# Three edits to a hybrid decoder trunk: the queue that begins a running sum, the order of the attention's output products, and the tick of two heads' transposes

## The chip, the cores and the metric

The kernel runs on one core of one Trainium2 chip. The metric is the device time of one execution in microseconds (us). The core's engines run side by side, each through its own instructions in order: TensorE (PE, matrix products; its weight loads are shown as PEld), VectorE (DVE), ScalarE (ACT), GpSimd (POOL) and SyncE (SP). SP and POOL here do little but begin DMA transfers, each on a queue of its own: SP's is "q1 hardware_dynamic" in the profile, POOL's "q0 software_dynamic".

## What is computed

Two layers, 512 tokens of width 1024, float32. Layer 0 mixes tokens with dilated attention (three groups of eight heads), layer 1 with a gated recurrence; each is followed by a feed-forward block (FFN) of width 3072. Cut to what matters:

```python
def reference(x, ...):
    for layer in range(2):
        h = rms_norm(x, norm_mix_pre[layer])
        h = dilated_attention_mixer(h, ...) if layer == 0 else rglru_mixer(h, ...)
        x = x + rms_norm(h, norm_mix_post[layer])
        h = conv_ffn(rms_norm(x, norm_ffn_pre[layer]), w_up, conv_w, conv_b, w_down)
        x = x + rms_norm(h, norm_ffn_post[layer])
    return x

def dilated_attention_mixer(x, w_qkv, w_o, rel_bias):   # the end of it
    alpha = softmax(lses, axis=0)                       # over the three head groups
    o = sum(alpha[..., None] * outs, axis=0)
    return o.reshape(B, S, 1024) @ w_o                  # output products

def conv_ffn(x, w_up, conv_w, conv_b, w_down):
    u = causal_dwconv(x @ w_up, conv_w, conv_b)
    g, v = u[..., :3072], u[..., 3072:]
    return (gelu(g) * v) @ w_down
```

## The kernel before

Every product is done in three passes of TensorE, because each operand is split in two parts: ACT makes the high part (`whi` for weights, L253; `ahi` for activations, L184) and DVE the low part (`wlo`, L265; `alo`, L185). A pass has 128 by 512 products, and one weight half of 1 MB gives two "units" (a unit is one `whi` and one `wlo` tile; eight are held, `W_UNITS`).

Some products are done by a scheme that needs seven products of blocks where plain code needs eight, and for it sums of blocks of the weights: a "first" block is copied from memory into a tile named `sum`, and then further blocks are added to it in place by DMA transfers that accumulate. `add_up` (L298) issues both: the copy at L309, the accumulating ones at L311, all from POOL. POOL waits for one to land before it issues the next, because the next reads the tile that the former wrote. Plain blocks of weights are loaded by `load` (L317) into tiles named `raw`, from SP (L340). `plan` lists all weights in the order of their use; `loads` (L280) is called whenever a tile was read, first issues the loads that have a free tile, then the next step of a sum. The entries of `plan` that belong to the attention have numbers below `state["lagging"]` (L1733), the FFN's and the recurrence's lie above.

In each FFN, 16 products (`step`, L971, products at L633, tile `vq`) of the down projection are woven between the blocks of the up projection (tile `ps`, L436); their weights come as `value` loads and as sums, in the order that `down_quarters` (L1696) gives: load; first and sum; load; sum; load; sum; first and sum; and the same again for a second unit. The sums of the up projection (`w_seven`, L414) have firsts of their own. There are 16 firsts above `lagging`: four of the up and four of the down projection in each layer.

Work that is not tied to one product runs as a "side": a generator that is resumed at `tick()`, which is called after each piece of products; `yield n` lets n ticks go by. The loads' splitting is pumped at ticks too.

At the end of the attention, `rows_run` (L694) does the output products in the order of `LAST_ORDER`: pairs of token tiles (four of 128 tokens) and chunks of `w_o` (four of 256 rows, two heads each). Each of its 16 pieces has 12 matmuls and ends in a tick. The tiles' products collect in `acc` tiles, two PSUM banks for each token tile; PSUM has eight banks (`pp`, L133), and all tiles named `ps`, `vq`, `acc`, `PT`, `O`, `tr` take theirs from these eight. The last four heads (numbers 4 to 7) are still being finished in the first ticks: `strided` (L1352) scales the weights `L` (L1429), and for the last two heads, with `ahead` set, writes the shares to memory (L1442), reads them spread (L1364), turns `L` on TensorE (L1449, tile `PT`, two banks for a head), copies the turned tiles out on ACT (L1451), and makes `oT` (L1465 to L1470). `prep` splits `oT` into `ahi` and `alo` up to two pieces ahead of their products.

Of the kernel before, what the change touches and what calls it, by code (L numbers as in the profile page):

```python
# [53 lines left out]


LAST_ORDER = [
    ([0, 1], [0, 1, 2]), ([2], [0]), ([0], [3]), ([1], [3]), ([3], [0]), ([2, 3], [1]), ([2], [2, 3]), ([3], [2, 3]),
]

LOCAL_STEPS = [("l", 0, 1), ("l", 1, 0), ("l", 1, 1), ("l", 2, 0), ("l", 2, 1)]  # L60
# [35 lines left out]
def kernel(  # L96
# [28 lines left out]
    nc = tc.nc  # L125
# [12 lines left out]
    def nm(s):  # L138
        uid[0] += 1
        return f"{s}{uid[0]}"  # L140

    def gen(dt=F32, s="g"):
        return gp.tile([P, 512], dt, tag="g", name=nm(s))

    def psum(s="ps"):
        return pp.tile([P, 512], F32, tag="ps", name=nm(s))
# [41 lines left out]
    state = {"raw": 0, "free": RAW_BUFS, "at": 0, "live": 0, "next": 0, "rows": False, "hold": False, "slots": 4, "tick": 0, "lagging": 0}  # L188
# [91 lines left out]
    def loads():  # L280
        moved = True
        while moved:
            moved = False
            while state["raw"] < len(plan) and plan[state["raw"]][0] in ADDED:
                state["raw"] += 1
            if state["raw"] < len(plan):
                kind = plan[state["raw"]][0]
                if state["slots"] >= SLOTS[kind] if kind in SLOTS else state["free"]:
                    load()
                    moved = True  # L290
            while total["next"] < len(plan) and plan[total["next"]][0] not in ADDED:
                total["next"] += 1
            i = total["next"]
            if i < state["raw"] and total["open"] and after[i] in finished:
                add_up(i)
                moved = True

    def add_up(i):  # L298

        kind, kd, cols, srcs = plan[i]  # L300
        if total["tile"] is None or total["cols"] != cols:
            total["cols"] = cols
            total["tile"] = cp.tile([P, 512 // cols, 4, cols], F32, tag="gain", name=nm("sum"))
        tile_, at = total["tile"], 0
        part = tile_[:, int(kind[-1] == "1")]
        for src, m in srcs:
            dst = part[:, :, at : at + m]
            if kind[:5] == "first":
                nc.gpsimd.dma_start(dst, src)  # L309
            else:  # L310
                nc.gpsimd.dma_start(dst, src, accum_op=ALU.add)  # L311
            at += m
        raws[i] = tile_ if kind == "mix" else part
        since[i] = state["tick"]
        total["next"] += 1
# [762 lines left out]
    def attention(hT, post, pre, spill):  # L1078
# [201 lines left out]
        def to_dram(t, ms, name):  # L1280
            d = dp.tile([P, 512], F32, name=name)
            nc.sync.dma_start(strips(d)[:, :, ms, :], strips(t)[:, :, ms, :])
            return d

        def from_dram(d, ms):

            t = gen(s="PT")
            w = 32 * (ms.stop - ms.start)
            src = bass.AP(tensor=d.tensor, offset=d.offset + 32 * ms.start, ap=[[P, P], [32 * 512, 4], [1, w]])
            dst = t.rearrange("p (i c) -> p i c", i=4)[:, :, 32 * ms.start : 32 * ms.stop]  # L1290
            nc.sync.dma_start(dst, src)
            return t.rearrange("p (i m q) -> p m i q", i=4, m=4)
# [59 lines left out]
        def strided(h, hh, qks, v, ahead=None):  # L1352
# [4 lines left out]
            def local_out():  # L1357
                t = gen(s="ow")
                nc.sync.dma_start(t, o0[h])
                return t  # L1360

            def spread(d):
                t = gen(s="share")
                nc.sync.dma_start(t, bass.AP(tensor=d.tensor, offset=d.offset, ap=[[0, P], [1, 512]]))  # L1364
                return t
# [74 lines left out]
            if ahead:  # L1440
                yield 1
                nc.sync.dma_start(cd, c0)  # L1442
                yield 1
                share = spread(cd)
                for L in Ls:
                    ps = psum("PT")
                    for r in range(4):
                        c = slice(r * P, (r + 1) * P)
                        nc.tensor.transpose(ps[:, c], L[:, c], ident)  # L1449
                    pt = gen(s="PT")  # L1450
                    nc.scalar.activation(pt, ps, AF.Copy)  # L1451
                    pts.append(pt.rearrange("p (r u) -> p r u", r=4))
            else:
                yield 1
                placed = [to_dram(t, all_, f"std{h}{gi}") for gi, t in enumerate(turned)]
                nc.sync.dma_start(cd, c0)
                yield 2
                pts = [from_dram(d, all_) for d in placed]
                share, ow = spread(cd), local_out()
# [69 lines left out]
        for hp in range(4):  # L1529
# [4 lines left out]
            for j in range(4):  # L1534
                if j == 3 and hp:
                    by_residue(vrows[hp], v)
                if j == 1 and last:
                    prep(2)
                if j == 2 and last:
                    both = [(qs[:2], ks[:2])]  # L1540
                    heads = [strided(6 + hh, hh, both, v, True) for hh in range(2)]
                    for hh, g in enumerate(heads):
                        side(one(g), 1 + hh)
                feat_tiles(1, hT, lambda m, ps: sink(2 * j + m, ps), paired=False)
                step("s", hp, j)
            if not hp:
                by_residue(vrows[hp], v)
            if last:
                both.append((qs[2:], ks[2:]))
                for hh, g in enumerate(heads):  # L1550
                    next(g)
                for hh in (1, 0):
                    side(heads[hh], 1 + hh, first=True)
                prep(4)
                for t in range(4):
                    xs_sb[t] = load_x(t)
            else:
                both = [(qs[2 * g : 2 * g + 2], ks[2 * g : 2 * g + 2]) for g in range(2)]
                for hh in range(2):
                    side(strided(2 * hp + hh, hh, both, v), 1 + hh)  # L1560
# [294 lines left out]
```

## Time and profile before

| | us |
|---|---|
| median of 3 runs | 1408.19 (1405.84 to 1410.74) |
| profiled execution, its own time | 1408.95 |
| its span, first to last instruction | 1407.2 |
| PE busy | 1364.2 |
| DVE busy | 1053.5 |
| ACT busy | 671.9 |
| POOL busy | 123.5 |

The profile is of one execution. The span is divided by engine into busy time and idle time; an idle time is put down to what ended it. The attention ends at about 492 us of the span, layer 0's FFN runs from there to about 870, the recurrence to about 1025, and layer 1's FFN to the end.

### The profile page before, as it was taken

What the parts mean: (1) busy time and instruction counts of PE and PEld (TensorE: products, weight loads), DVE (VectorE), ACT (ScalarE), POOL (GpSimd) and SP (SyncE); (2) the same over time, 40 slices, a digit from 0 to 9 for tenths busy, and PEclk for the clock granted to TensorE, in tenths of its full rate; (3) what the DMA queues carried; (4) which work ended last, traced back from release to release, by engine and by line L of the source; (5) the groups of instructions that cost most, each with busy time, mean ns of one, the idle gap of its engine ahead of it and who ended that gap; (6) DMA issues with size and microseconds to landing.
All of it is one profiled execution on the core that took longest, in us unless ns stands there. A gap on an engine that the chain in (4) does not pass through costs nothing.

```text
span 1407.2 us, 18680 instructions
## 1 busy us (share of the span) xinstructions
PE 1364.2 (97%) x7109; PEld 1201.2 (85%) x7109; DVE 1053.5 (75%) x1838; ACT 671.9 (48%) x1125; POOL 123.5 (9%) x141
## 2 busy tenths in 40 slices
PE   8999999999998999998999999999999999999997
PEld 5888888888887899997878879888899997888886
DVE  6886483737585788877949689878979877968785
ACT  6334342423444554445535354579563445535351
POOL 1211011011010001000000020000000010000020
PEclk9999999999999999999999999999999999999999
DMA  8979669686838244573658775233153672758771
GB/s 247 238 219 280 171 186 256 204 204 160 283 128 289 88 151 110 162 193 90 194 160 195 199 209 180 90 120 120 61 165 82 174 206 65 187 165 216 185 219 60
DMA packets 179116, 243.10 MB, mean 173 GB/s; under 512 B 16632, under 2 KB 131840, under 8 KB 179026
## 3 DMA queue, kind: packets, MB, share of 16 engines
q1 hardware_dynamic: 143008, 172.23, 37.5%
q0 software_dynamic: 36016, 69.67, 23.6%
q8 instruction: 56, 0.92, 0.3%
q14 instruction: 34, 0.28, 0.1%
q10 hardware_dynamic: 2, 0.00, 0.0%
HBM read 218.23 MB, written 28.36 MB: 175 GB/s over the span
## 4 chain that ended last, share of the span: by engine, by line
DVE 29%; DMA 11%; ACT 9%; PE 5%; issue 5%; DVEq 0%; SPq 0%; ACTq 0%; POOLq 0%
DVE wlo L265 9%; DVE u L821 7%; DMA sum<-in_ffn_w_down_dram 5%; PE acc L436 4%; ACT whi L253 3%; DMA raw<-in_ffn_w_down_dram 2%; DMA raw<-in_ffn_w_up_dram 2%; ACT u L817 2%; DVE xb L1574 1%; ACT u L831 1%; DVE A L915 1%; DVE y L647 1%; DVE u L833 1%; DVE c L647 1%; DVE run L608 1%
## 5 line engine op out<-in xcount | busy, mean ns | idle before, releaser
L436 PE MATMUL ps<-hT,whi 128*128 128x512 f32 (+1 forms) x2528 | 696.9, 362 | 0.8 <-DVE hT L499 0.6
L436 PEld LDWEIGHTS ps<-hT,whi 128*128 128x128 f32 x2528 | 458.9, 190 | 57.5 <-issue 1.3
L436 PE MATMUL ps<-hT,wlo 128*128 128x512 f32 (+1 forms) x1264 | 456.3, 361 | 3.0 <-DVE wlo L265 3.0
L253 ACT ACTIVATE whi<-raw 128x1024 fp32r<-128x1024 f32 x233 | 239.1, 1052 | 149.5 <-DMA raw<-in_attn_w_qkv_dram 73.5
L265 DVE TENSOR_TENSOR wlo<-raw,whi 128x1024 fp32r<-128x1024 f32 x233 | 280.3, 1218 | 30.6 <-ACT whi L253 30.4
L436 PEld LDWEIGHTS ps<-hT,wlo 128*128 128x128 f32 x1264 | 239.6, 190 | 32.7 <-DVE wlo L265 5.0
L821 DVE SCALAR_TENSOR_TENSOR u<-ps,cols,u 128x511 f32<-128x511 f32 (+1 forms) x160 | 119.6, 747 | 88.3 <-ACT u L817 85.4
L633 PE MATMUL vq<-whi,A 128*128 128x512 f32 x448 | 140.5, 385 | 2.6 <-ACT A L922 2.6
L253 ACT ACTIVATE whi<-sum 128x1024 fp32r<-128x1024 f32 x68 | 70.7, 1049 | 142.4 <-DMA sum<-in_attn_w_qkv_dram 74.2
L265 DVE TENSOR_TENSOR wlo<-sum,whi 128x1024 fp32r<-128x1024 f32 x68 | 82.0, 1218 | 49.1 <-ACT whi L253 49.1
L436 PE MATMUL acc<-whi,ahi 128*128 128x512 f32 x256 | 98.8, 386 | 2.7 <-ACT ahi L184 2.7
L436 PE MATMUL acc<-whi,alo 128*128 128x512 f32 x256 | 97.9, 382 | 3.4 <-DVE alo L185 3.3
L633 PEld LDWEIGHTS vq<-whi,A 128*128 128x128 f32 x448 | 86.0, 192 | 16.0 <-ACT A L922 3.4
L436 PE MATMUL acc<-wlo,ahi 128*128 128x512 f32 x256 | 97.9, 383 | 1.5 <-DVE wlo L265 1.5
L633 PE MATMUL vq<-wlo,A 128*128 128x512 f32 x224 | 87.1, 389 | 9.6 <-DVE wlo L265 9.6
L831 ACT ACTIVATE u<-u 128x512 f32<-128x512 f32 x48 | 30.3, 631 | 111.4 <-DVE u L821 111.4
L817 ACT ACTIVATE u<-ps,cols 128x512 f32<-128x512 f32 x80 | 61.1, 764 | 4.7 <-PE ps L436 4.7
L633 PE MATMUL vq<-whi,T 128*128 128x512 f32 x192 | 59.7, 382 | 0.0
L436 PEld LDWEIGHTS acc<-whi,alo 128*128 128x128 f32 x256 | 48.6, 190 | 12.5 <-DVE alo L185 5.8
L633 PEld LDWEIGHTS vq<-wlo,A 128*128 128x128 f32 x224 | 43.1, 192 | 18.5 <-DVE wlo L265 12.4
L436 PEld LDWEIGHTS acc<-whi,ahi 128*128 128x128 f32 x256 | 48.7, 190 | 9.8 <-ACT ahi L184 3.3
L436 PEld LDWEIGHTS acc<-wlo,ahi 128*128 128x128 f32 x256 | 48.7, 190 | 9.6 <-DVE wlo L265 3.1
(246 smaller groups left out, 1799.2 us busy)
## 6 DMA issues: line engine op xcount, KB each, us to landing
raw<-in_ffn_w_up_dram SPq DMA_DIRECT2D x44, 1024.0 KB
raw<-in_attn_w_qkv_dram SPq DMA_DIRECT2D x25, 1024.0 KB
sum<-in_ffn_w_down_dram POOLq DMA_DIRECT2D x24, 1024.0 KB, 8.6
raw<-in_ffn_w_down_dram SPq DMA_DIRECT2D x16, 1024.0 KB
sum<-in_attn_w_qkv_dram POOLq DMA_DIRECT2D x24, 512.0 KB, 8.1
raw<-in_attn_w_qkv_dram SPq DMA_DIRECT2D x16, 512.0 KB
sum<-in_ffn_w_up_dram POOLq DMA_DIRECT2D x16, 512.0 KB, 6.8
raw<-in_lru_w_in_dram SPq DMA_DIRECT2D x8, 1024.0 KB
```

What stands on the lines that cost most here:

```text
L253: nc.scalar.activation(hi, raw, AF.Copy)
L265: nc.vector.tensor_tensor(lo, raw, hi.bitcast(F32), op=ALU.subtract)
L436: mm(dst, l[a], r[b], start=start and n == 0, stop=stop and n == 2)
L608: nc.vector.tensor_tensor(r[h], a, b[:, k], op=ALU.add if sg > 0 else ALU.subtract)
L633: mm(banks[u], act(a)[:, 2 * j + k, u * P : (u + 1) * P], woven(W[b][:, k, :]), start=(j, k, n) == (0, 0, 0), stop=(j, k, n) == (1, 1, 2),)
L647: nc.vector.tensor_tensor(dst[u], a[u], b[u], op=op)
L817: nc.scalar.activation(u, ps, AF.Identity, scale=cc[:, j : j + 1], bias=cc[:, 48 + j : 49 + j])
L821: nc.vector.scalar_tensor_tensor(u[:, d:], ps[:, : S - d], wc, u[:, d:], op0=ALU.mult, op1=ALU.add)
L831: nc.scalar.activation(u, u, AF.Gelu_apprx_tanh)
L833: nc.vector.tensor_tensor(gv[k], gv[k], u, op=ALU.mult)
L915: nc.vector.tensor_tensor(run[:, k], run[:, k] if prior is None else prior[k], src[k], op=ALU.add if sign > 0 else ALU.subtract,)
L1574: nc.vector.scalar_tensor_tensor(u[:, d:], ps[:, : S - d], wc, u[:, d:], op0=ALU.mult, op1=ALU.add)
```

## The change

Three edits:

- `LAST_ORDER`: the pieces of token tiles 0 and 1 with chunk 2 (heads 4 and 5) move from the fifth and sixth place to the seventh and eighth. Token tile 2 takes chunks 0 and 1 (heads 0 to 3) in the fifth and sixth place, and tile 3 takes both at the eleventh and twelfth. There are 16 pieces as before. Chunk 3 comes to tiles 0 and 1 at the ninth and tenth place (eighth and ninth before).
- `add_up`: the "first" copies of entries above `lagging` are issued from SP, not from POOL. Those of the attention stay on POOL, as do all accumulating transfers.
- `strided` with `ahead`: two ticks instead of one go by between the writing of the shares and their reading with the transposes. So the transposes of heads 6 and 7 come after the fourth and fifth piece, not after the third and fourth, and their `oT` one tick later too.

```diff
 LAST_ORDER = [
-    ([0, 1], [0, 1, 2]), ([2], [0]), ([0], [3]), ([1], [3]), ([3], [0]), ([2, 3], [1]), ([2], [2, 3]), ([3], [2, 3]),
+    ([0, 1], [0, 1]), ([2], [0, 1]), ([0, 1], [2]), ([0], [3]), ([1], [3]), ([3], [0, 1]), ([2], [2, 3]), ([3], [2, 3]),
 ]
@@ add_up
             if kind[:5] == "first":
-                nc.gpsimd.dma_start(dst, src)
+                (nc.gpsimd if i < state["lagging"] else nc.sync).dma_start(dst, src)
             else:
                 nc.gpsimd.dma_start(dst, src, accum_op=ALU.add)
@@ strided
             if ahead:
                 yield 1
                 nc.sync.dma_start(cd, c0)
-                yield 1
+                yield 2
                 share = spread(cd)
```

## Rows read from the trace of the kernel before

**Rows 1.** The page: busy time by engine, and what the slices moved.
```profile
PE 1364.2 (97%) x7109; PEld 1201.2 (85%) x7109; DVE 1053.5 (75%) x1838; ACT 671.9 (48%) x1125; POOL 123.5 (9%) x141
GB/s 247 238 219 280 171 186 256 204 204 160 283 128 289 88 151 110 162 193 90 194 160 195 199 209 180 90 120 120 61 165 82 174 206 65 187 165 216 185 219 60
```
**Rows 2.** PE's waits, 430 to 600 us: total us, times, longest.
```profile
PE acc L436 <- ACT ahi L184: 2.7, 2, 2.3
PE PT L1449 <- DVE L L1429: 2.3, 1, 2.3
```
**Rows 3.** PE's waits, 600 to 830 us.
```profile
PE vq L633 <- DVE wlo L265: 5.8, 3, 3.3
PE ps L436 <- DVE wlo L265: 2.1, 2, 1.6
PE vq L633 <- ACT A L922: 0.7, 1, 0.7
```
**Rows 4.** PE's waits, 1130 to 1380 us.
```profile
PE vq L633 <- DVE wlo L265: 3.8, 4, 1.6
PE vq L633 <- ACT A L922: 1.8, 1, 1.8
...
PE ps L436 <- DVE wlo L265: 0.9, 2, 0.6
```
**Rows 5.** Stretches: length, busy us of each engine (instructions), granted PE clock, DMA.
```profile
660.30:663.70 3.40, 3.40 (x10) 2.68 (x9) 3.14 (x6) 3.22 (x5) 1.28 (x1) 0.50 0.32 46
664.00:704.00 40.00, 40.00 (x187) 35.04 (x186) 37.22 (x55) 22.01 (x28) 2.08 (x2) 1.00 0.72 192
```
**Rows 6.** The chain of waits: start us, us (DMA: issue to landing), what.
```profile
615.87 10.68 DMA raw<-in_ffn_w_down_dram
...
698.47 6.30 DMA sum<-in_ffn_w_down_dram
...
705.17 13.22 DMA sum<-in_ffn_w_down_dram
...
727.74 9.38 DMA raw<-in_ffn_w_up_dram
...
1148.92 11.36 DMA raw<-in_ffn_w_down_dram
```
**Rows 7.** SP in order of time: start us, us, line, what it issues.
```profile
620.31 0.37 SPq L340 DMA_DIRECT2D raw<-in_ffn_w_up_dram  x1
...
688.78 0.37 SPq L340 DMA_DIRECT2D raw<-in_ffn_w_up_dram  x1
```
**Rows 8.** ACT in order of time; in brackets the idle time before, and its end.
```profile
644.52 1.04 ACT L253 ACTIVATE whi<-sum 128x1024 fp32r<-128x1024 f32 x1
...
688.51 1.06 ACT L253 ACTIVATE whi<-sum 128x1024 fp32r<-128x1024 f32 x1 [0.73 <-DMA sum<-in_ffn_w_down_dram]
...
694.06 1.06 ACT L253 ACTIVATE whi<-raw 128x1024 fp32r<-128x1024 f32 x1 [2.31 <-DMA raw<-in_ffn_w_up_dram]
...
808.13 1.06 ACT L253 ACTIVATE whi<-sum 128x1024 fp32r<-128x1024 f32 x1 [15.04 <-DMA sum<-in_ffn_w_down_dram]
...
1178.25 1.04 ACT L253 ACTIVATE whi<-sum 128x1024 fp32r<-128x1024 f32 x1
```
**Rows 9.** POOL in order of time, around the FFN's sums of layer 0.
```profile
608.41 0.79 POOL L309 DMA_DIRECT2D sum<-in_ffn_w_down_dram  x1 [13.37 <-DVE wlo L265]
...
679.89 1.30 POOL L311 DMA_DIRECT2D sum<-in_ffn_w_down_dram  x1 [18.28 <-DVE wlo L265]
...
793.80 1.27 POOL L311 DMA_DIRECT2D sum<-in_ffn_w_down_dram  x1 [6.21 <-DMA sum<-in_ffn_w_down_dram]
```
**Rows 10.** PE and ACT in order of time, at the attention's end.
```profile
451.43 1.63 PE L1449 MATMUL PT<-ident,L 128*128 128x128 f32 x8 [2.26 <-DVE L L1429]
...
453.38 0.63 ACT L184 ACTIVATE ahi<-oT 128x512 fp32r<-128x512 f32 x1 [4.40 <-DVE oT L1469]
453.91 1.07 ACT L1451 ACTIVATE PT<-PT 128x512 f32<-128x512 f32 x2
```

## The prediction

> **What bounds the kernel now.** I read the page first: PE is busy for 97% of the span, DVE for 75% [rows 1]. So at most the idle 43 us of PE are to be had, and the question is which of its waits the change touches. The waits of PE by stretch tell that. At the attention's end there are 2.7 us for ACT's split of activations, two waits with 2.3 the longest, and 2.3 us for DVE's scaling of a head's weights [rows 2]. In layer 0's FFN there are 8.6 us: 5.8 and 2.1 for the low parts of weights, 0.7 for an operand [rows 3]. In layer 1's there are 6.5 us of the same kinds [rows 4]. A long wait costs more than itself: after the one of 3.3 us PE ran 3.4 us at the lower of its two clocks, granted 0.50, that is 1.2 GHz; ten matmuls took what 16 take at 2.4 GHz (187 in 40 us, 0.214 us each) [rows 5]. That is another 1.7 us. There are three such dips behind waits, at 452, 660 and 1172 us, of which one row stands.
>
> The chain of waits then tells why the weights are late. ACT works strictly in order, so one split that waits for a transfer holds the convolutions behind it, and DVE, which waits for those. A load begun at 615.87 takes 10.68 us to land, its twin in layer 1 takes 11.36, the sum begun at 705.17 takes 13.22, a load at 727.74 takes 9.38 [rows 6]. A load of the same size with no other transfer beside it, begun at 688.78 [rows 7], is read from 694.06 on, just when it lands: 5.28 us [rows 8]. A sum alone takes 8.6 us, from 679.89 [rows 9] to 688.51; the slowest here 14.3, from 793.80 [rows 9] to 808.13 [rows 8].
>
> **Edit 1: 16 firsts on SP.** Nothing is added or removed; each first leaves POOL's queue (0.79 us of POOL [rows 9]) and takes 0.37 us of SP's [rows 7]. What counts is where it stands. The eight of the up projections cost nothing: where their weights are used PE waits for none (in layer 0 from 492 to 600 us, where [rows 2] has no wait for weights). A sum that came later than its lead would cost PE the difference. The eight of the down projection come in four kinds, once in each layer. Loads are issued ahead of a step of a sum in the same call, and SP's instructions run in order, so a first stands behind all loads written before it.
>
> (a) The first at 608.41 [rows 9] was written after the loads of 615.87 [rows 6] and 620.31 [rows 7], which wait for their tiles. POOL ran ahead of them; SP can't. The first is issued at about 620.7, 12 us later, and neither it nor its sum runs beside the load of 615.87 any more. This load then lands in 5.28 us instead of 10.68: 5.4 us earlier, and ACT and DVE gain that lead. The price is the sum. The load of 620.31 lands at 625.6; the first, next in the same queue, moves its 1.05 MB at the 289 GB/s of the best slice [rows 1] in 3.6 us and lands at 629.2; the sum is issued at about 629.6 and takes 8.6 to 14.3 us, say 11: it lands at 640.6 (638.2 to 643.9). ACT now comes to it at 644.52 without waiting [rows 8], then at 639.1. So 3.9 us of lead are left (5.4 to 0.6). PE's waits here are 0.7 and, 20 us on, 3.3 with the dip of 1.7 [rows 3, 5]. The first goes; PE then needs 4.0 of lead to lose the other. Worth 5.7 in full, 0.6 with the least lead; I take 5.2. Layer 1: the load gains 11.36 − 5.28 = 6.1; its successor is issued 4.5 us behind it, as in layer 0, so the first lands at about 1162.3 and the sum at 1173.7 (1171.3 to 1177.0), where ACT comes at 1178.25 − 6.1 = 1172.2 [rows 6, 8]. The wait of 1.8 and its dip of 1.7 come before the sum and go; the wait of 1.6 [rows 4] then needs 5.1 of lead and finds 4.6 (6.1 to 1.3). I take 4.6; between 1.3 and 5.1.
>
> (b) The first at 698.47 took 6.30 us from POOL [rows 6]. SP's queue is empty then, so it starts at the same time and lands in 5.28: its sum begins 1.0 us earlier, and ahead of the load that now crowds it. Of 2.5 us of waits (5.8 less 3.3 [rows 3]) I take 2.0, between 1.0 and 2.5. In layer 1 POOL's first is quicker already, by 0.7 us; 0.8 of some 1.8, not under 0.4.
>
> (c) A first is written just after the load of 727.74, and POOL's copy runs beside that load. Behind it, the load lands in 5.28 instead of 9.38 [rows 6], and the 2.1 us of waits for its low part go [rows 3]; but the first lands 2.9 us later than now (727.74 + 5.28 + 3.6 against 727.25 + 6.3), and so its sum. PE takes that sum's product without a wait today, but no row shows by how much. I take 1.2, between −2.9 and 2.1; in layer 1 0.4 of 0.9 [rows 4], down to −2.9.
>
> (d) The last first, at 786 us, meets an empty SP queue again: its sum, for which ACT idles 15.04 us [rows 8], begins about a microsecond earlier. PE's waits behind it are split among many operands: 1.0 for both layers, between −1 and 2.
>
> The Trainium skill speaks against this edit, on the page "DMA: Bandwidth & Descriptors", section "Issuing engines are not separate DMA queues": transfers of all issuing engines interleave on the same 16 DMA engines, so that another issuer saves only the time to issue. The row agrees that they share (10.68 against 5.28 us); by that rule alone edit 1 would be worth nothing, and the rival "same" below is its case.
>
> **Edits 2 and 3: the attention's end.** Piece 3 waits 2.3 us for ACT [rows 2]; its operand and its place stay, so this wait stays. The wait of 2.3 us ahead of head 7's transposes [rows 10] is what the edits aim at: one more piece (12 × 0.214 = 2.6 us) comes ahead of them, on heads that are long ready. But the piece is tile 2's, and opens two more banks: six of eight are held by sums then, and the other two by head 6's turned weights. Head 7's transposes need these two back, and ACT frees them with the copies of 453.91. Those stand behind a split that waits for DVE until 453.38 [rows 10], and nothing moves that. So PE goes on at about 454.5 instead of 451.43; the second copy ends at 455.0, four more transposes take 0.8 us at most (half of 1.63), and PE is through at 455.7, one piece ahead. Now it has done the same work at 453.1 + 2.6 + 1.5 (most of the dip) = 457.2. That is 1.5 us gained; but the wait is then 2.5 us, and a dip behind it gives 1.7 back. The smaller wait for ACT (2.7 less 2.3 = 0.4 us [rows 2]) goes, since the table load no longer stands between head 7's output and its split. I take 1.0: 4.5 if no bank is waited for (2.3 + 1.7 + 0.4), −1.2 if the dip comes and the later ticks are late. Tile 0's and 1's norms start one piece later, and three pieces still cover their transposes; if that cover were gone, PE would wait for ACT as in [rows 2], 0.4 to 2.3 us. SP's instructions in `strided` are the same; the spread read, which waits for its write, no longer stands ahead of the other head's write.
>
> **Sum.** 5.2 + 4.6 + 2.0 + 0.8 + 1.2 + 0.4 + 1.0 + 1.0 = 16.2 us off the profiled execution's 1408.95: 1392.8. That execution is 0.8 us above the median of the three runs, so 1392 for a median. All best ends together give 24.6 us, 1384; all worst ends −4.7, 1413.
>
> **Rivals.** *Sums too late.* The lead of (a) is eaten by the later sum (14.3 us, as the slowest today), (b) to (d) give their low ends without a loss: 0.6 + 1.3 + 1.0 + 0.4 + 0.5 = some 4 to 6 us, 1403. For it: the sum comes 12 us later. Against: even then it lands before the time at which ACT comes today.
>
> *Same.* The transfers only share the engines, and whichever is begun first pays: the load still meets other traffic, DVE's own work (37.2 of 40 us busy behind the dip [rows 5]) refills every lead, and the attention's wait only moves. Then the time is 1407 to 1408. Against: the load of 615.87 has nothing left beside it until it lands. This is the case of the rule cited above.
>
> *Slower.* SP's queue hands out three transfers without overlap, 5.28 us each: in (a) the first lands 15.8 us behind the first load, at 631.7, and with a sum of 14.3 us at 646.4, later than ACT's 644.52 of today by 1.9; in layer 1 by about 1.1. In (c) the first lands at 738.3, 4.7 later than now; with a slack of 2 for PE there, each layer loses 2.7. Together 8.4 us, less the 1.4 of (b)'s low ends: 1415. It decides from the point at which the sum of (a) lands behind 644.5, 15 us after a first that lands at 629.2; no sum here took that long.
>
> **How the numbers follow.** The forecast (10 to 25 us off, 1384 to 1399): 0.62. Sums too late (1399 to 1404): 0.17. Same: 0.13. Slower: 0.08. A measurement of this kernel tells about 0.3%, 4.2 us, from no change: faster means below 1404, 0.79; same 0.14; slower 0.07. The range, 1384 to 1404, takes in the first two cases and so both ends of most unknown costs.
>
> **What would show it.** Right, if SP issues the first copies at about 620 and 1153 us; if the loads ahead of them land in 5 to 6 us instead of 10.68 and 11.36; if PE's waits of 0.7 and 3.3 us, 1.8 and 1.6 us, and both dips of the clock, are gone; if head 7's transposes wait for ACT's copies and not for DVE. Wrong, if ACT now waits for the sum that it reads at 644.52 for more than some 2 us, if the load's 10.68 us hardly shrink, or if SP's queue holds a first for long and the loads behind it come late.

## The result and the profile after

The changed kernel takes 1385.37 us in the median of three runs (1384.54 to 1386.12), where the kernel before took 1408.19 beside it. The ratio is 0.9837 with a 95% interval of 0.9808 to 0.9866: some 23 us less (18.9 to 27.0). The profiled execution took 1385.37 us, of which the span is 1383.6. In later runs the same two kernels gave 1383.87 and 1402.99, a ratio of 0.9864 (0.9831 to 0.9896), 19.1 us less (14.6 to 23.7). Both intervals hold 18.9 to 23.7 us.

The page: PE's busy time fell by 7.4 us against [rows 1] with the same 7109 instructions (two dips of its clock that went, below, are part of that), and POOL has 16 instructions fewer.

```profile
PE 1356.8 (98%) x7109; PEld 1200.9 (87%) x7109; DVE 1052.2 (76%) x1838; ACT 670.7 (48%) x1125; POOL 111.1 (8%) x125
```

PE's waits from 430 to 600 us, to be read against [rows 2] (total us, times, longest):

```profile
PE tr L489 <- DVE xs L481: 3.4, 2, 2.6
PE acc L436 <- ACT ahi L184: 2.4, 1, 2.4
PE PT L1449 <- ACT PT L1451: 1.5, 1, 1.5
```

The wait for DVE ahead of PT has gone, and one for ACT's copies stands there. But a line that [rows 2] does not have, 3.4 us for `xs`, is larger than what went. From 600 to 830 us, against the 8.6 us of [rows 3], this is the whole list:

```profile
PE vq L633 <- DVE wlo L265: 2.5, 2, 1.6
```

From 1130 to 1380 us no wait is listed any more, where [rows 4] had 6.5 us. So the feed-forward layers gave the time, and the attention did not.

Their transfers, in the chain of waits (start, us from issue to landing); against [rows 6] the load of 615.87 takes 5.64 us instead of 10.68, but the sum of 705.17 is as slow as it was:

```profile
616.16 5.64 DMA raw<-in_ffn_w_down_dram
...
693.06 6.40 DMA sum<-in_ffn_w_down_dram
700.11 13.08 DMA sum<-in_ffn_w_down_dram
```

SP, POOL and ACT in order of time at the first of these places, against [rows 7 to 9]: the first transfer stands behind both loads on SP, POOL issues the sum at 629.11, and ACT comes to that sum 0.84 us before it has landed.

```profile
620.58 0.37 SPq L340 DMA_DIRECT2D raw<-in_ffn_w_up_dram  x1
621.05 0.52 SPq L309 DMA_DIRECT2D sum<-in_ffn_w_down_dram  x1
...
629.11 1.28 POOL L311 DMA_DIRECT2D sum<-in_ffn_w_down_dram  x1 [33.56 <-DMA sum<-in_ffn_w_down_dram]
...
640.72 1.06 ACT L253 ACTIVATE whi<-sum 128x1024 fp32r<-128x1024 f32 x1 [0.84 <-DMA sum<-in_ffn_w_down_dram]
```

Three stretches as in [rows 5] (behind the colon the length, then busy us of PE, PEld, DVE, ACT and POOL, PE's granted clock, the DMA share). Of the three dips of the clock the one at the attention's end is left, behind the wait of 2.4 us; at 660 and 1172 us, where the kernel before ran at 0.50, the clock is full:

```profile
443.00:447.00 4.00, 3.92 (x10) 2.85 (x11) 3.77 (x12) 3.49 (x5) 0.00 (x0) 0.57 1.01 401
...
660.00:663.00 3.00, 3.00 (x15) 2.62 (x15) 1.50 (x3) 1.34 (x2) 0.00 (x0) 1.00 1.13 203
1172.00:1175.00 3.00, 3.00 (x15) 2.64 (x14) 2.73 (x5) 3.00 (x8) 0.22 (x1) 1.00 0.00 0
```

**Gains by place.** All kernels here run the same 7109 matmuls, outside the attention's end in the same order. The start of the n-th matmul in one trace, less that in the first trace of the kernel before, shows where time is gained. The table is worked out that way from all traces of this case: us gained in each stretch. (a) to (d) are the prediction's four places of the down-projection; in layer 0, (b) and (c) run into each other. "att" is 405 to 513 us of the kernel before, (a) 513 to 697 and 1134 to 1240, (b) and (c) 697 to 789 and 1240 to 1309 (in layer 1 divided at 1270), (d) 789 to 875 and 1330 to 1399. The recurrence between the two layers is left out; it moves by −1.6 to 0.4 us.

```
                            att   0a  0b+c   0d    1a   1b   1c   1d
kernel before, again       -0.2  0.2   0.1 -0.1  -0.6  2.1  0.1  1.5
e23  (edits 2 and 3)       -1.1 -1.4   0.6  3.5  -1.9  1.9 -0.1  1.8
e2   (edit 2)              -1.7  2.0  -0.6  2.7  -0.2  2.1 -0.3  0.7
e3   (edit 3)              -2.9  0.1   0.5  0.2  -0.3  1.1  0.1  0.1
a_only                     -0.3  6.3   0.4  3.5   6.3  1.3  0.1  0.9
pool_late                   1.3  4.6  -0.4  0.2   6.3  1.6  0.1  0.2
ahead                       0.8  3.9   2.4  3.5   3.8  1.7  1.1  2.3
c_only                      0.1  0.2   2.5  2.3  -1.7  2.4  1.4  0.8
bd_only                    -0.2  0.6   4.6  3.5  -2.1  2.4  1.4  2.3
e1   (edit 1)               1.4  6.3   5.7  3.5   6.3  2.4  1.4  2.3
v    (change, other order) -2.2  6.3   2.6  3.5   6.3  2.4  1.4  2.3
changed kernel             -1.8  6.3   2.7  3.3   6.3  2.4  1.4  2.3
changed kernel, again      -0.6  6.3   2.9  3.5   6.3  2.4  1.4  2.3
```

Read it by columns. A place is the change's when its column has the same number wherever the edit is made, well outside what it shows in kernels that leave the place alone. 0a and 1a are such places: 6.3 in all five traces with the edit, −1.4 to 2.0 and −2.1 to 0.0 without it. So one entry is good to about 2 us, and an entry says more when several traces agree on it. 0d and 1b are not such places: several kernels that leave them alone "gain" there as much. This one table is what most of the following rests on.

### The profile page after: what moved, and what is told of

It reads as the page before. It is cut to its first block, busy times and chain, and to the rows that moved or that the text cites. A ratio compares the mean times of both kernels' runs of the same rounds, so it can differ in the third digit from the quotient of the medians.

```text
span 1383.6 us, 18693 instructions
## 1 busy us (share of the span) xinstructions
PE 1356.8 (98%) x7109; PEld 1200.9 (87%) x7109; DVE 1052.2 (76%) x1838; ACT 670.7 (48%) x1125; POOL 111.1 (8%) x125
## 4 chain that ended last, share of the span: by engine, by line
PE 38%; DVE 18%; ACT 6%; DMA 3%; issue 2%; DVEq 0%; ACTq 0%; POOLq 0%; SPq 0%
PE ps L436 20%; PE vq L633 8%; PE acc L436 7%; DVE wlo L265 4%; DVE u L821 3%; PE vq L436 3%; ACT whi L253 2%; DMA sum<-in_ffn_w_down_dram 1%; DVE xb L1574 1%; DVE run L608 1%; DVE x L551 1%; ACT u L817 1%; DVE u L833 1%; ACT u L831 1%; DVE post L546 1%
```

## The experiments

The expectations count from the first runs' 1408 us. In the later runs the kernel before took 1401 to 1405, so each result is given against the kernel before of the same runs.

### Edit 1 alone, and edits 2 and 3 alone

e1 has the changed line of `add_up`, with the attention as before; e23 has the other two edits, with `add_up` as before.

> The first transfers of the sums outside the attention on the sync queue, the attention left as before. Theory (the transposes of tiles 2 and 3 give back what the attention's two edits gain): the whole gain is in the feed-forward layers, so this kernel comes out like the changed kernel, 1384 to 1387 us, with the PT wait of 2.3 us at 451, the 2.7 us for ahi and the clock dip at 452 still there, and no wait over 1.2 us for xs at the transposes of tiles 2 and 3. Rival (the attention's edits are worth the 1.0 us that was forecast, or up to 4.5): 1386.5 to 1390 us.

Measured: 0.9856 (0.9831 to 0.9881), 20.2 us less than 1403.85, the gain of the whole change. PE's waits at the attention's end are those of the kernel before, and from 590 to 815 us its list of waits is empty:

```profile
PE PT L1449 <- DVE L L1429: 2.3, 1, 2.3
PE acc L436 <- ACT ahi L184: 1.9, 2, 1.4
PE tr L489 <- DVE xs L481: 1.0, 1, 1.0
```

The ahi wait was 1.4 us at the longest and not 2.3; this wait is different in nearly every trace.

> The attention's two edits together, all sums on the GpSimd queue as before. Theory (gain and loss cancel): 1406 to 1410 us, no difference that can be told; the trace shows the PT wait on VectorE gone, one of 1.5 us on ScalarE's copies in its place, and 2.5 to 3.5 us of waiting for xs at the transposes of tiles 2 and 3 that the kernel before doesn't have. Rival (1.0 to 4.5 us gained): 1403.5 to 1407.5 us, the xs waits of tiles 2 and 3 at most 1.2 us as before.

Measured: 1.0003 (0.9988 to 1.0019), 0.4 us slower and not to be told from no change; the interval leaves the rival no more than 1.7 us of its 1.0 to 4.5. The trace has the list that the theory expected:

```profile
PE tr L489 <- DVE xs L481: 3.5, 2, 2.7
PE acc L436 <- ACT ahi L184: 1.9, 1, 1.9
...
PE PT L1449 <- ACT PT L1451: 1.3, 1, 1.3
```

So edit 1 carries the change, and alone it can't be told from it (0.9856 against 0.9837 and 0.9864). But e23's own columns 0d, 1b and 1d show 3.5, 1.9 and 1.8 us of gain at places that it does not touch; what they are is taken up below. The eight first transfers of the up projections, which edit 1 moves too, were not moved by themselves.

### The attention's two edits apart, and a third order

> The new order of the output products alone; the last transposes PT are where they were. If it is the order that delays the norms of tiles 0 to 3 (tile 0's sum is finished one piece later), the xs waits at the transposes of tiles 2 and 3 are here too, 2.5 to 3.5 us together, while the PT wait on VectorE of about 2.3 us is still there: 1408 to 1412 us, some 1 to 3 slower than before. Rival (the xs waits come from the transposes PT that move one step on): the xs waits at most 1.2 us, 1406 to 1409 us.

Measured: 1.0006 (0.9991 to 1.002), 0.8 us slower. The xs waits were 3.5 us, as the theory said; the PT wait was 0.8 us, not 2.3. Head 7's transposes began at 451.73, hardly later than before (451.43), but PE came to them later, after a wait of 2.6 us and matmuls at a lower clock (0.62 granted from 443 to 447). The order is not the reason: c_only and bd_only, below, have the attention of the kernel before and a PT wait of 0.8 us too.

> The last transposes PT one step on, with the old order of the output products. If the order alone delays the norms, this keeps the gain without the loss: the PT wait on VectorE is gone, xs waits at tiles 2 and 3 at most 1.2 us, 1404 to 1407 us; the price is a later split of the seventh and eighth head, at most 1 us of waiting ahead of the output products that need it. Rival (the later transposes hold up the output products of heads 6 and 7 and so all norms): a wait of 2 us or more for PT's copies at these products, 1408 to 1412 us.

Measured: 1.0051 (1.0036 to 1.0066), 7.2 us slower. The theory fell and the rival held: with the old order, the product that now comes ahead of head 7's transposes is one with heads 4 and 5, and it waits 4.64 us for the low part of their split. (The rival had named PT's copies.)

```profile
453.44 0.79 PE L436 MATMUL acc<-whi,alo 128*128 128x512 f32 x1 [4.64 <-DVE alo L185]
457.86 1.64 PE L1449 MATMUL PT<-ident,L 128*128 128x128 f32 x8
```

Only 2.9 of the 7.2 us stand in the table's column "att"; where the rest was lost is open.

The two edits belong together: the later transposes need a product that is ready ahead of them, and the new order gives one. v takes the changed kernel and puts only one such product ahead:

```
-    ([0, 1], [0, 1]), ([2], [0, 1]), ([0, 1], [2]), ([0], [3]), ([1], [3]), ([3], [0, 1]), ...
+    ([0, 1], [0, 1]), ([2], [0]), ([0, 1], [2]), ([0], [3]), ([1], [3]), ([3], [0]), ([2, 3], [1]), ...
```

> The changed kernel with another order of the output products: tile 2 with the first heads only goes ahead of the fifth and sixth, its third and fourth stay behind, so that tile 0 is finished at the eighth product, as in the kernel before. Theory (the norms start when tile 0 is finished, and what the transposes gained was lost at tiles 2 and 3 because it is finished one product later): the PT wait is 1.5 us as in the changed kernel, the xs waits of tiles 2 and 3 fall from 3.4 to 1 to 1.5 us, and the whole is 1 to 2.5 us faster than the changed kernel. Rival (the product of tile 0 with the fifth and sixth heads, now one place earlier, waits for their split): a new wait of 1 us or more there for alo, and no gain.

Measured: 0.9875 (0.9855 to 0.9896), 17.5 us less; no faster than the changed kernel. The xs waits fell to 1.0 at this place, as the theory said, but a wait of 2.04 us came up in their place, and not where the rival had put it: at tile 0's product with heads 6 and 7.

```profile
467.27 0.48 PE L436 MATMUL acc<-whi,ahi 128*128 128x512 f32 x1 [2.04 <-ACT ahi L184]
```

What sets the attention's end is then seen by two rows of each kernel: where DVE begins the norm of tile 0, and where PE can begin tile 3's transposes. The kernel before (its second trace):

```profile
469.49 0.69 DVE L546 TENSOR_TENSOR post<-acc,gain 128x512 f32<-128x512 f32 x1 [1.30 <-ACT junk L443]
...
502.52 1.08 PE L489 MATMUL tr<-ident,xs 128*128 128x128 f32 x8 [1.11 <-DVE xs L481]
```

The changed kernel:

```profile
470.40 0.69 DVE L546 TENSOR_TENSOR post<-acc,gain 128x512 f32<-128x512 f32 x1 [1.29 <-ACT junk L443]
...
503.30 1.08 PE L489 MATMUL tr<-ident,xs 128*128 128x128 f32 x8 [2.61 <-DVE xs L481]
```

They are 33.0 and 32.9 us apart, and 32.9 to 33.0 in every trace here but v's (34.1). The norms of the four tiles are one chain on DVE and ACT, which begins when tile 0's sum is complete. PE reaches tile 3 sooner than that and waits, for 1.1 or for 2.6 us; by these rows the end is the same. Tile 0 in turn isn't complete before head 7's split: v's product waits for it, and in the kernel before the same product already waits 0.44 us, at 467.19. So the old order seems to be within half a microsecond of what an order can reach here, as long as head 7 is not ready sooner; that is argued from these rows, and no order but this, the changed one and v's was tried. The changed order does tile 0 ninth instead of eighth: in the column "att" its four traces (e23, e2 and two of the changed kernel) lose 0.6 to 1.8 us, where the eight with the old order and the old step lie between −0.3 and 1.4.

### Place (a): order or queue

In a_only a down-projection's first goes to SP at one place of each layer and to POOL at the others (`place` counts them):

```
-                nc.gpsimd.dma_start(dst, src)
+                (nc.sync if place and place in "a" else nc.gpsimd).dma_start(dst, src)
```

> Of the first transfers of the down-projection's sums, only the first of each layer (the one that shared its time with two loads) goes to the sync queue; all others stay on the GpSimd queue. Theory (this one place in each layer is worth 6.3 us, as the changed kernel's trace has it): 12.5 us faster than the kernel before, a ratio of about 0.991; no wait for wlo or A in the first 50 us of either feed-forward layer over 0.8 us. Rival (the moves share the same slack, so that one alone only shifts the wait to the next place): 5 to 9 us faster.

Measured: 0.9933 (0.9907 to 0.9958), 9.4 us less (5.9 to 13.0), which holds the theory's 12.5 and most of the rival's 5 to 9. The table decides: 6.3 and 6.3 us at its two places, the theory's number (which came from the same first trace of the kernel before), and PE's list of waits from 600 to 700 us is empty. The trace also has 3.5 us at (d) in layer 0 and 1.3 and 0.9 at (b) and (d) in layer 1, all untouched.

Is it the queue that helps, or the order? pool_late leaves the transfer with POOL and holds it there until the newest load has landed; ahead leaves it on SP and issues it before the loads.

```
+                if place == "a":
+                    seen = small(1)
+                    nc.gpsimd.tensor_copy(seen, newest[-1][:, 0, 0:1])
                 nc.gpsimd.dma_start(dst, src)
```

> All sums on the GpSimd queue as before, but the first transfer of the first down-projection weights of each layer is held there until the newest load has landed, by a copy of one column of that load on GpSimd ahead of it. Theory (order): the two loads run alone again, and 9 to 12.5 us of the change's gain come back without any transfer moved to the sync queue. Rival (queue): within 2 us of the kernel before.

Measured: 0.9944 (0.9923 to 0.9966), 7.8 us less; by the table 4.6 and 6.3 us at the place, 10.9 of 12.6. POOL's copy waits for the load of 620; then come the first and the sum, 4.8 and 3.7 us later than in the changed kernel:

```profile
625.11 0.54 POOL L317 COPY s<-raw 128x1 f32<-128x1 f32 x1 [30.38 <-DMA raw<-in_ffn_w_up_dram]
625.83 0.80 POOL L318 DMA_DIRECT2D sum<-in_ffn_w_down_dram  x1 [0.18 <-DVE u L831]
632.79 1.28 POOL L320 DMA_DIRECT2D sum<-in_ffn_w_down_dram  x1 [6.17 <-DMA sum<-in_ffn_w_down_dram]
```

The load that stood beside the sum is quick here too (chain of waits), and ACT waits for the sum instead (its waits from 600 to 660 us):

```profile
615.48 4.92 DMA raw<-in_ffn_w_down_dram
...
ACT whi L254 <- DMA sum<-in_ffn_w_down_dram: 4.1, 1, 4.1
```

What is missing in layer 0 goes with the 3.7 us by which the sum starts later (632.79 against 629.11): PE has two waits for low parts here, 1.1 us together, where a_only has none.

```
             i = total["next"]
+            if state["lagging"] <= i < min(len(plan), state["raw"] + 4) and plan[i][0] == "first" ...:
+                add_up(i)
             while state["raw"] < len(plan) and plan[state["raw"]][0] in ADDED:
                 state["raw"] += 1
```

> The first transfers on the sync queue as in the change, but that of the first down-projection weights of each layer is issued ahead of its two loads, not behind them. Theory (order: it is worth something only because the loads that the matrix units wait for go first and alone): the second load lands about 5 us later again, and 8 to 12 of the 12.5 us of these two places are lost, so 11 to 15 us faster than the kernel before. Rival (queue: the transfer itself costs less on a hardware queue than on GpSimd's): all is kept, 21 to 24 us faster.

Measured: 0.9907 (0.9884 to 0.993), 13.0 us less, in the theory's 11 to 15 and far from the rival's 21 to 24. But the edit does more than its text says: its condition holds at (c) too, where the first is issued at 719.93 and its load at 721.04. So the total is that of two places, and the columns 0b+c and 1c are lower too (2.4 and 1.1, where e1 has 5.7 and 1.4). By the table (a) keeps 3.9 and 3.8 of 6.3 and 6.3 us: 4.9 lost, less than the 8 to 12 of the text. At (a) the first, issued at 605.56, has landed before the loads begin and costs them nothing; it is the sum that runs beside them now, and the second load, which the theory named, takes the 9.93 us:

```profile
605.56 0.37 SPq L314 DMA_DIRECT2D sum<-in_ffn_w_down_dram  x1
613.39 0.37 SPq L345 DMA_DIRECT2D raw<-in_ffn_w_down_dram  x1
...
613.42 1.28 POOL L316 DMA_DIRECT2D sum<-in_ffn_w_down_dram  x1 [20.71 <-DVE wlo L265]
...
617.79 9.93 DMA raw<-in_ffn_w_up_dram
```

So at (a) it is the order. Late on POOL's queue is nearly as good as late on SP's; early on SP's is worse. SP is only the cheapest way to be behind the loads: its order needs no wait. The control was made at this place alone.

### Places (b), (c) and (d)

> Of the first transfers of the down-projection's sums, only the third of each layer goes to the sync queue, behind the load that it shared its time with. Theory (the place is worth what the traces with and without it show, 2.4 to 2.7 us in the first layer and 1.4 in the second): 3.5 to 4.5 us faster, a ratio of 0.997. Rival (the forecast's 1.2 and 0.4): 1.6 us, a ratio of 0.999.

Measured: 0.9965 (0.9949 to 0.998), 4.9 us less. The interval (2.8 to 7.2) holds the theory's 3.5 to 4.5 and not the rival's 1.6. The table has 2.5 in layer 0 and 1.4 in layer 1. The first now stands behind the load, and the sum behind both:

```profile
728.06 0.46 SPq L314 DMA_DIRECT2D sum<-in_ffn_w_down_dram  x1
...
737.33 8.26 DMA sum<-in_ffn_w_down_dram
```

> Of the first transfers of the down-projection's sums, only the second and the fourth of each layer go to the sync queue. Theory (most of what the first two traces showed at these two places was chance): 1 to 3 us faster than the kernel before, a ratio of 0.998 to 0.999. Rival (the difference of the first two traces at these places is the change's: 3.3 and 2.3 at the fourth, 0 and 2.4 at the second): 7 to 8 us, a ratio of 0.9945.

Measured: 0.9943 (0.9921 to 0.9965), 8.0 us less (4.9 to 11.1): the rival's number, and the theory fell. By the table (b) and (c) in layer 0 give 4.6 us together although (c) is not touched, (d) gives 3.5 and 2.3. In layer 1, too, 1c has the 1.4 us that c_only has. So (b) and (c) share slack: where (b) is quick, the waits at (c) shrink (in layer 0 from 2.1 to 0.6 us), and what the two give by themselves can't be added.

Two kernels that were run again unchanged show what chance there is:

> The kernel before, unchanged, once more. Theory (part of the difference of the two first traces was chance: the waits near the end of the first feed-forward layer and ahead of the third quarter of the second are there in some executions and not in others, whatever the change): this trace lacks some of the waits of 0.4, 0.7 and 1.7 us at 831 to 842, as three kernels with unchanged transfers of that place already lacked them, and its waits differ from the first trace's by 2 to 5 us in sum. Rival (they belong to the kernel before): the same waits to 0.3 us.

Measured: a ratio of 1.0004 (0.9986 to 1.0022). At the end of layer 0's feed-forward the waits of the first trace are all there again, so the theory fell for this place (820 to 850 us):

```profile
PE acc L436 <- DVE alo L185: 1.6, 1, 1.6
PE acc L436 <- DVE wlo L265: 1.2, 2, 0.7
```

In layer 1, 2.1 and 1.5 us at (b) and (d) had gone without any edit, so there it held.

> The changed kernel, unchanged, once more, timed beside the kernel before on one chip. Theory (about 19 us are the change's, the rest of the 24 us between the two first traces was chance): a ratio of 0.985 to 0.988, 17 to 21 us. Rival (all of it is the change's): 0.982 to 0.984, 22.5 to 25 us. The trace has no wait over 0.3 us for wlo, A or alo in either feed-forward layer but the two at about 717 and 721.

Measured: 0.9864 (0.9831 to 0.9896), 19.1 us, in the theory's range; the interval reaches the rival's. The trace has the waits that were expected and no others: two at (b) in layer 0, 2.2 us together. Its columns are those of the changed kernel's first trace to 0.2 us in both layers.

Neither "chance" nor "the change" is the whole answer for (b) and (d): the places are on a tipping point. Two rows of POOL and SP at (b), layer 0. The changed kernel:

```profile
700.11 1.28 POOL L311 DMA_DIRECT2D sum<-in_ffn_w_down_dram  x1 [23.95 <-DMA sum<-in_ffn_w_down_dram]
...
700.50 0.38 SPq L340 DMA_DIRECT2D raw<-in_ffn_w_down_dram  x1
```

e1, where the first was issued at 693.25 and landed in 5.9 us instead of 7.0 (from its issue to the sum's):

```profile
699.14 1.28 POOL L311 DMA_DIRECT2D sum<-in_ffn_w_down_dram  x1 [22.79 <-DMA sum<-in_ffn_w_down_dram]
...
700.70 0.38 SPq L340 DMA_DIRECT2D raw<-in_ffn_w_down_dram  x1
```

The sum is issued 0.39 us ahead of the next load in the one, 1.56 in the other; it takes 13.1 us in the one and 10.0 in the other, and PE's two waits of 2.5 us together are there or not. The DMA queues tell why (packets, MB, share of the 16 engines; q1 holds SP's transfers, q0 the sums). In the changed kernel the packets from 701.0 to 705.4 are these, in e1 those from 701.0 to 704.3 are the ones below:

```profile
q1 hardware_dynamic: 438, 0.90, 73.0%
```

```profile
q0 software_dynamic: 267, 0.55, 101.3%
```

Whichever transfer's packets come first has the engines alone for 3 to 4 us in these two traces: the load's begin at 701.57 in the changed kernel and the sum's at 705.50; in e1 the sum's at 701.14 and the load's at 704.34. And a sum's packets begin 2.0 us behind its issue (e1), a load's 1.1 (the changed kernel), so that a sum has to be issued some 0.9 us ahead to be first. In the other traces it is the same at (b) and (d): at a lead of 0.88 us and less the load's packets come first, at 0.99 and more the sum's, and the first has 0.8 to 4.7 us alone, the less the nearer the lead is to 0.9. The same over all 14 traces, at (b) and (d) of both layers, by the time from the sum's issue to that of the next load:

```
sum ahead of the next load by   cases   the sum takes, us
under 0.9 us                      15    12.6 to 14.3
0.9 to 1.4 us                     11    10.6 to 12.4
over 1.4 us                       30     9.5 to 12.2
```

All cases of the first line are in layer 0. There, at (d), a first on POOL was followed by its sum 6.0 to 7.1 us later, and the sum fell on either side; on SP it was 5.5 to 6.0 us, and the sum was ahead by over 2 us in all six traces. So at (d) the edit makes sure of what came in half of the traces without it. PE's time goes with it: of the eight traces with POOL's first at (d), the four whose sum took 14.0 to 14.3 us have −0.1 to 0.2 in column 0d, and the four whose sum took 10.4 to 12.0 us have 2.3 to 3.5. The rows at (d), layer 0, are these in the kernel before (its sum was issued at 793.80 [rows 9]) and, below, in the changed kernel, where the sum takes 9.9 us:

```profile
794.61 0.37 SPq L340 DMA_DIRECT2D raw<-in_ffn_w_down_dram  x1
```

```profile
787.01 1.28 POOL L311 DMA_DIRECT2D sum<-in_ffn_w_down_dram  x1 [21.08 <-DMA sum<-in_ffn_w_down_dram]
...
789.56 0.37 SPq L340 DMA_DIRECT2D raw<-in_ffn_w_down_dram  x1
```

Here, then, the queue counts and not the order: the first stands behind nothing on either queue, and from SP its sum can follow about a microsecond sooner. At (b), SP's first took 5.9 to 7.4 us and did not make sure of it: quick in e1, bd_only and nearly in ahead, slow in both traces of the changed kernel and in v. These three carry the attention's edits and the first three don't; whether that is the reason was not tried. No run moved a sum's lead and nothing else, so for (b) and (d) the tipping point rests on the agreement of these 56 cases.

## Why the prediction was right, point by point

The forecast was 1392, in a range of 1384 to 1404; the time is 1385.4, near the good end. The mechanism held; several sizes did not, and two steps failed.

**(a), 5.2 and 4.6 forecast, 6.3 and 6.3 measured** (a_only and the four traces with the whole edit 1 agree to 0.1). The steps are as forecast: first issued at 621.05 (said 620.7), sum at 629.11 (629.6), landed by 640.7 (640.6), the load in 5.64 and 4.93 us in two traces (5.28). What had stood beside that load was the sum alone: in the kernel before the first had landed at 614.3. Mis-sized was what PE would lose: all waits and both dips went, though I had held that the lead was too small to clear layer 1's last wait; its 6.3 us lie outside my 1.3 to 5.1. The waits and the dip that I counted were 5.7 in layer 0. The starts of the single matmuls hold most of the rest: behind each wait PE is some 0.26 us later than the wait's own length (3.57 us behind the one of 3.3). In layer 1 there is also a wait of 0.4 us that I left out. And the first trace was a mild one there: its longest wait for a low part is 1.6 us, where the second trace of the kernel before has one of 3.3. Against the mean of the seven traces that leave (a) alone (0.2 and −1.0) the place is worth 6.1 and 7.3.

**(b), 2.0 and 0.8 forecast.** Layer 0 is the step that failed: "it starts at the same time and lands in 5.28: its sum begins 1.0 us earlier, and ahead of the load that now crowds it". The first landed in 6.40 us, the sum was 0.39 us ahead of that load and took 13.08, and 2.5 us of waits stayed. e1 and bd_only show that the step is right where the first lands in time. In layer 1 the table has 2.4 us, but 1.1 to 2.4 in seven traces that leave the place alone: against their mean with the first trace of before, 1.6, some 0.8 is the edit's. That this is the forecast's number is luck: it had been worked out from waits of 1.8 us in one trace.

**(c), 1.2 and 0.4 forecast, 2.5 and 1.4 measured by itself.** The bound of −2.9 for a later first (3.1 by its own terms, 736.6 against 733.55) was empty. In c_only the first is issued at 728.1 and its sum only at 737.3, 3.3 us later than before, but while the sum's packets run, from 739.3, no load's do until 744.2: it takes 8.3 us instead of 11.4 and lands at 745.6, where it landed at 745.3. I had moved the start of the sum and kept its duration. Some of the 1.4 us in layer 1 comes without this edit as well: bd_only has them.

**(d), 1.0 forecast for both layers.** Against the mean of the eight traces with POOL's first (1.5 in layer 0, 0.75 in layer 1) the gains of 3.5 and 2.3 leave about 3.5. Mis-sized: I counted the microsecond by which the first lands earlier, not the 4.4 us by which layer 0's sum is shorter when it comes ahead of the load (9.86 against 14.25). In layer 1 the sum was ahead before, too, and took 10.8 instead of 11.9.

**The attention, 1.0 forecast (−1.2 to 4.5), a loss of some 1 to 2 by the table.** Timed by itself, e23 lost 0.4 us (2.7 lost to 1.7 gained). The banks were seen rightly: PT waits 1.5 us for ACT's copy (3.0 in the second trace), not for DVE. What failed is "three pieces still cover their transposes". That was true of tiles 0 and 1, which wait for nothing, and beside the point: the wait came at tiles 2 and 3, whose norms stand behind tile 0's in one chain of 33 us. I had asked what covers the next step, not what the end hangs on.

**The sum of terms.** With the sizes measured: 12.6 for (a), 2.8 for (b) and (c) in layer 0, 0.8 and 1.4 in layer 1, 3.5 for (d), −1 for the attention: 20.1 us, where the two timings of the change gave 22.8 and 19.1 and e1 20.2. The forecast had 16.2: (a), (c) and (d) were sized too low, (b) in layer 0 and the attention too high, which took back a part of the miss. The three parts timed by themselves give 9.4, 8.0 and 4.9, 22.3 in all, which is no closer a check, as (b) and (c) share slack.

**The rivals.** "Sums too late" did not occur: ACT waits 0.84 us for the sum of (a). It did in pool_late, whose sum was 3.7 us later and which lost 1.7 of 6.3 us in layer 0. "Slower" did not either. "Same" fell. The Trainium skill, page "DMA: Bandwidth & Descriptors", section "Issuing engines are not separate DMA queues", says that another issuer saves only the time to issue. pool_late agrees with its ground: from POOL the place is worth 10.9 of 12.6 us. But the conclusion that I drew, that the edit is then worth nothing, does not hold: the issuer also decides what a transfer stands behind (at (a) and (c)), and the time that it saves (about a microsecond until the sum can follow, at (d)) can decide which of two transfers is first. Edit 1 is made of these two, 20.2 us in e1.

## What to carry to other kernels

Before moving a transfer to another queue, ask what it will stand behind and what will run beside it before you ask which queue is faster: a copy that nobody waits for yet belongs behind the loads that are waited for. Where two transfers are issued within a microsecond of each other, look which is first in several traces; if that changes, the place is a tipping point, and one trace's wait there is neither the change's nor the kernel's. When a wait in front of a serial chain is removed, measure from the chain's start: here 33 to 34 us behind tile 0, whatever PE did in between.

## What the runs showed of the hardware

Two transfers of 1 MB, a load and an accumulating one, issued within 1.6 us of each other did not share the engines from the start: the one whose packets came first kept the other's out for 3 to 4 us (438 packets of one queue and none of the other, or 267 and none); over the 14 traces, at (b) and (d), it was 0.8 to 4.7 us. From then on both moved side by side (358 and 361 packets from 705.5 to 711 in the changed kernel). And a sum issued 0.39 us ahead of a load was still second. The Trainium skill, page "DMA: Bandwidth & Descriptors", section "SWDGE vs HWDGE vs iDMA", has each engine go round-robin between its queues; the second stretch agrees with that, the first 3 to 4 us do not show it, and no run here says why. So how long an accumulating transfer of 1 MB takes, 8.0 to 14.3 us here, hangs mostly on whether a load is just ahead of it (12.6 to 14.3), just behind (9.5 to 12.4), or away (8.3 in c_only). A first that waits behind a load in its own queue shows 8 to 10 us from its issue to its sum's issue, instead of 5.5 to 7.4, and by a_only and c_only that cost PE nothing.
